# Shifted load buffers, two more of them, an earlier load of the output weights and a shorter split-ahead in a fused transformer kernel

## The chip, the cores and the metric

One core of one Trainium2 chip runs the whole program. The time is device microseconds of one execution. The kernel before was timed three times: 1851.71, 1855.15 and 1855.19 us, median 1855.15 us. One more execution was recorded by the hardware profiler; it took 1854.01 us, and all rows below are from it.

## The reference

Two blocks in a row on 256 tokens of 1024 features, all in fp32:

```python
def first_block(x, c, ada_w, ada_b, ...):
    mod = (silu(c) @ ada_w + ada_b)              # six segments of 1024
    sh1, sc1, g1, sh2, sc2, g2 = split(mod, 6)
    h = rms_norm(x, ln1_g) * (1 + sc1) + sh1
    x = x + g1 * hybrid_mixer(h, w_in, w_out, ...)   # NSA heads and MoBA heads, then @ w_out
    h = rms_norm(x, ln2_g) * (1 + sc2) + sh2
    x = x + g2 * sparse_moe(h, router_w, w1, w2, ...)  # 32 experts, the top 4 of each token
    return x

def sparse_moe(...):    # per expert e and its tokens
    u = hf[toks] @ w1[e] + b1[e]                 # 1024 x 2048
    y = ((lin + 1) * g_ * sigmoid(1.702 * g_)) @ w2[e] + b2[e]   # 1024 x 1024
```

The second block puts 16 learned tokens in front (272 in all) and runs two layers: stick-breaking attention with a squared-ReLU MLP, then a gated linear recurrence with another such MLP, and a last norm.

## The kernel before, in words

Weights are read from HBM once, in one fixed order, by the class `Stream` (from L140). An **item** is one load of 1 MiB into a load buffer of 128 partitions x 2048 fp32; most items are cut into two **units**. `pump` (its DMA is L169, all on SP's queue) issues items in their order. The buffers stand in a ring, and the next item is issued as soon as the ring's first buffer holds only an item that lies before `base`, the first item not yet wholly used. `widen(places, until)` puts more buffers in front of the ring until item number `until`. Dense weights are used as a pair of fp32r tensors: `split_to` writes a unit's high part with a cast on ScalarE (L189) and the rest with a subtraction on VectorE or GpSimd (L191). `get`, called at each use of a unit, first splits up to `ahead` units beyond it, and those two instructions go into the in-order queues of ScalarE and VectorE at that point of the program; where the unit's load has not landed, both queues stand still. `get_raw` hands out an item without a split (modulation and expert weights).

Three stages follow each other:

- **Mixer**, 0 to 251 us (`pre`, `mixer`, `route`). `ada` computes the six segments of the modulation, each from four items (quarters, matmul L436, copy L440); segments 1 and 0 come first, the others are worked off in pieces between other work by `side_to`. `dense_t` and `dense_v` multiply the normed input by the columns of `w_in` (each product three matmuls, L289 to L291 or L488 to L490). The compressed keys and values go through `hid` (matmul L628, copy L632); the norm of a query or key ends with matmul `hb` (L717) and the product `z` (L719). Attention follows, then `w_out`, the router, and the ranks of the tokens within each expert.
- **Experts**, 251 to 1195 us. 17 jobs, 15 of them two experts side by side. A job gathers its tokens (matmul L1407 of a 0/1 matrix `S` with the normed rows, held as `h2h` and `h2l`; scaled and shifted at L1409 into `xs`), multiplies by `w1` (L1442, 8 items for each expert), applies the gate, multiplies by `w2` (L1535, 4 items for each expert) and adds into `h` (L1558 to L1563). There are nine such gathers of eight tiles. 384 items are read. The first 16 are known before the routing; which experts the others hold is read from `ids`.
- **Second block**, 1196 to 1852 us: dense products from split weights. Its first norm (`norm_in`) makes eight `hn_hi` on ScalarE, eight `hn_lo` on VectorE (L1628), eight squares (L1638 on GpSimd, L1640 on ScalarE), and adds them in two chains (L1647, L1650).

The load ring holds four buffers of its own; three arena buffers (r1 to r3) are added until the attention, later the arena tiles that the routing sets free and five split tiles. Scratch tiles of the mixer live in the same arena: `acc` in s4, `alibi` in s6, `z` in r0 and r1, `xn`, `h2h`, `h2l` in s2, s3, s4.

## Time and profile before

| what | value |
|---|---|
| median of three runs | 1855.15 us (1851.71 to 1855.19) |
| profiled execution | 1854.01 us, span 1851.9 us |
| TensorE busy | 1724.2 us, 93% of the span |
| VectorE, ScalarE, GpSimd busy | 718.1, 525.4, 270.6 us |
| bytes moved | 549.63 MB, mean 297 GB/s |

The span runs from the first to the last instruction; the execution's own time is 2.1 us longer. A busy share is an average over the three stages, which have different limits, so the rows below are from short stretches. In a timeline row the first two numbers are the start and the duration in us (of the whole group where xN stands at the end), and a bracket gives the idle time of the engine just before and what ended it. PEclk is the clock granted to TensorE, as a share of its higher level (1.00 is 2.4 GHz, 0.50 is 1.2 GHz).

### The profile page before, as it was taken

The page shows a single profiled execution, that of the slowest core. Times are in us where ns is not written, and L with a number is a line of the kernel's source. Part 1 is how long each engine was busy: PE and PEld are TensorE (multiplying, and loading weights), DVE is VectorE, ACT ScalarE, POOL GpSimd, SP SyncE. Part 2 cuts the span into 40 slices and gives each one's busy share as a digit, 9 for nine tenths or more (in the row PEclk, how much of TensorE's full clock was granted, in tenths as well). Part 3 has the DMA queues.
Part 4 walks back from the last instruction along what each step waited for, and adds up shares of the span by engine and source line. Part 5 has one row for each costly group of instructions (what it writes and reads, how often), then busy time and mean ns, then how long its engine had stood idle before and what let it go on. Part 6 is the DMA issues. An engine that isn't in the chain of part 4 may idle for free. (4 is left out here: it accounts for less than half of the span.)

```text
span 1851.9 us, 25047 instructions
## 1 busy us (share of the span) xinstructions
PE 1724.2 (93%) x9964; PEld 1084.6 (59%) x9964; DVE 718.1 (39%) x1252; ACT 525.4 (28%) x953; POOL 270.6 (15%) x231
## 2 busy tenths in 40 slices
PE   6898989998999999998899989799999999989998
PEld 3776743332334333343443333388889999879986
DVE  3455631322222222221222212355575534876622
ACT  4443320000000000000000000246665544856633
POOL 0000020000000000000000000174433343004442
PEclk7999989999999999999999999999999999999999
DMA  9923889999999999999999999852246555446551
GB/s 344 344 73 114 271 335 398 421 420 422 421 422 421 421 422 420 421 421 421 421 422 420 422 421 421 339 179 81 80 137 180 176 169 173 136 128 182 188 192 72
DMA packets 166952, 549.63 MB, mean 297 GB/s; under 512 B 8656, under 2 KB 101840, under 8 KB 117488
## 3 DMA queue, kind: packets, MB, share of 16 engines
q1 hardware_dynamic: 166208, 546.02, 77.0%
q0 software_dynamic: 432, 1.57, 0.3%
q8 instruction: 80, 1.31, 0.3%
q10 hardware_dynamic: 192, 0.40, 0.1%
q14 instruction: 40, 0.33, 0.0%
HBM read 546.91 MB, written 1.05 MB: 296 GB/s over the span
## 5 line engine op out<-in xcount | busy, mean ns | idle before, releaser
L191 POOL TENSOR_TENSOR wsp<-wraw,wsp 128x1024 fp32r<-128x1024 f32 x91 | 220.0, 2420 | 442.7 <-ACT wsp L189 417.8
L1442 PE MATMUL u<-wraw_s,xs 128*64 128x512 f32 (+1 forms) x848 | 248.6, 600 | 7.3 <-DMA wraw_s<-in_exp_w 7.2
L289 PE MATMUL dps<-hn_hi,wsp 128*128 128x272 f32 (+1 forms) x816 | 239.8, 294 | 7.9 <-DVE gt L2120 3.6
L189 ACT CAST wsp<-wraw 128x1024 fp32r<-128x1024 f32 x210 | 217.1, 1042 | 101.3 <-PE f L2175 46.9
L290 PE MATMUL dps<-hn_lo,wsp 128*128 128x272 f32 (+1 forms) x816 | 235.6, 289 | 4.6 <-DVE hn_lo L1628 4.4
L291 PE MATMUL dps<-hn_hi,wsp 128*128 128x272 f32 (+1 forms) x816 | 235.4, 288 | 0.2 <-DVE wsp L191 0.2
L191 DVE TENSOR_TENSOR wsp<-wraw,wsp 128x1024 fp32r<-128x1024 f32 x119 | 150.9, 1275 | 131.8 <-ACT wsp L189 131.6
L1442 PE MATMUL u<-wraw,xs 128*64 128x512 f32 (+1 forms) x600 | 178.9, 613 | 2.0 <-DMA wraw<-in_exp_w 1.9
L1442 PE MATMUL u<-wraw_r,xs 128*64 128x512 f32 (+1 forms) x600 | 178.5, 602 | 1.4 <-DMA wraw_r<-in_exp_w 1.3
L289 PEld LDWEIGHTS dps<-hn_hi,wsp 128*128 128x128 f32 x816 | 155.9, 191 | 13.3 <-issue 4.9
L290 PEld LDWEIGHTS dps<-hn_lo,wsp 128*128 128x128 f32 x816 | 155.8, 191 | 6.6 <-DVE hn_lo L1628 5.9
L291 PEld LDWEIGHTS dps<-hn_hi,wsp 128*128 128x128 f32 x816 | 155.9, 191 | 0.5 <-DVE wsp L191 0.5
L1442 PEld LDWEIGHTS u<-wraw_s,xs 128*64 128x64 f32 (+1 forms) x848 | 72.1, 140 | 120.7 <-issue 98.6
L1563 DVE SCALAR_TENSOR_TENSOR h<-cb,vec,h 128x256 f32<-128x256 f32 x136 | 59.3, 479 | 178.8 <-PE cb L1559 178.8
L1469 ACT ACTIVATE sg<-gl 128x1024 f32<-128x1024 f32 x17 | 18.0, 1057 | 386.1 <-DVE gl L1468 386.1
L1418 POOL CAST pk<-P 128x128 fp32r<-128x128 f32 x17 | 5.3, 311 | 813.4 <-PE u L1444 810.4
L1535 PE MATMUL y<-wraw,at 128*64 128x512 f32 (+1 forms) x360 | 112.6, 606 | 10.7 <-DMA wraw<-in_exp_w 10.7
L1535 PE MATMUL y<-wraw_s,at 128*64 128x512 f32 (+1 forms) x336 | 108.4, 597 | 11.5 <-DMA wraw_s<-in_exp_w 8.0
L1535 PE MATMUL y<-wraw_r,at 128*64 128x512 f32 x328 | 103.9, 596 | 13.4 <-DMA wraw_r<-in_exp_w 13.4
L1544 DVE SCALAR_TENSOR_TENSOR y<-y,gs 128x1024 fp32r<-128x1024 f32 (+1 forms) x18 | 22.0, 1224 | 215.2 <-ACT y L1543 203.4
L1409 DVE TENSOR_SCALAR xs<-gp,a,vec 128x256 f32<-128x256 f32 (+1 forms) x72 | 37.9, 527 | 164.4 <-PE gp L1407 164.3
L1543 ACT ACTIVATE y<-y,gs 128x1024 fp32r<-128x1024 f32 (+1 forms) x18 | 19.2, 1067 | 245.5 <-PE y L1535 245.5
(499 smaller groups left out, 2903.4 us busy)
## 6 DMA issues: line engine op xcount, KB each, us to landing
wraw_s<-in_exp_w SPq DMA_DIRECT2D x148, 1024.0 KB, 19.8
wraw<-in_exp_w SPq DMA_DIRECT2D x120, 1024.0 KB, 19.8
wraw_r<-in_exp_w SPq DMA_DIRECT2D x116, 1024.0 KB, 19.8
wraw<-in_mlp_w_up SPq DMA_DIRECT2D x32, 1024.0 KB, 5.5
wraw<-in_mlp_w_down SPq DMA_DIRECT2D x32, 1024.0 KB, 4.9
wraw<-in_ada_w SPq DMA_DIRECT2D x14, 1024.0 KB, 5.5
wraw<-in_sb_w_qkv SPq DMA_DIRECT2D x12, 1024.0 KB, 5.5
wraw_r<-in_ada_w SPq DMA_DIRECT2D x10, 1024.0 KB, 11.9
```

The costliest lines, as they stand in the source:

```text
L189: nc.scalar.copy(out=hv, in_=src)
L191: e.tensor_tensor(out=lv, in0=src, in1=lr, op=ALU.subtract)
L289: mm(o, lhsT=wh, rhs=xh, start=first, stop=False)
L290: mm(o, lhsT=wh, rhs=xl, start=False, stop=False)
L291: mm(o, lhsT=wl, rhs=xh, start=False, stop=last)
L1409: nc.vector.tensor_scalar(out=xs[:, k, 0:tot], in0=g, scalar1=self.a2[:, k:k + 1], scalar2=self.mod[:, 24 + k:25 + k], op0=ALU.mult, op1=A ...
L1442: mm(u[n][js], lhsT=xs[:, k, o + j * C:o + j * C + C], rhs=w[:, ns], start=(k == 0), stop=(k == 7))
L1469: nc.scalar.activation(out=sg, in_=g, func=AF.Sigmoid, scale=1.702)
L1535: mm(y[n][js], lhsT=at[:, k, js], rhs=w[:, cs], start=(k == 0), stop=(k == 7))
L1543: nc.scalar.activation(out=yh[:, a], in_=x, func=AF.Copy, scale=gs)
L1544: nc.vector.scalar_tensor_tensor(out=yl[:, a], in0=x, scalar=gs, in1=yh[:, a].bitcast(F32), op0=ALU.mult, op1=ALU.subtract)
L1563: nc.vector.scalar_tensor_tensor(out=h[:, m, META:NT], in0=o, scalar=self.mod[:, 40 + m:41 + m], in1=h[:, m, META:NT], op0=ALU.mult, op1=A ...
```

## The change

- The one-column tile `eps` takes 104 columns. It stands ahead of the load buffers and the arena in each partition, so all of these move from 128 bytes past a multiple of 512 to a multiple of 512.
- The order of the items: modulation segment 0 ahead of the first columns of `w_in` instead of behind; the first two items of `w_out` right behind the last columns of `w_in`, ahead of the four quarters of segment 3; then the other two items of `w_out`, each ahead of two quarters of segment 5.
- One more load buffer, s4, from the start until those last items (`late`); another, s3, from the MoBA projections to the second block. For this `acc` and `alibi` share s6, two small tiles lie in unused columns of `vvt`, and the normed rows are one fp32 tile `h2` in s4 instead of `xn`, `h2h` and `h2l`.
- `ahead` becomes 4 just before the attention rather than in the second product of `w_in`; before it is 2.
- The rows of `h2` are made by two instructions on ScalarE and two on VectorE, instead of six on ScalarE, two on VectorE and two on GpSimd. The gather is two fp32 matmuls a tile instead of four fp32r ones.
- The first norm of the second block: all eight squares on ScalarE, all sums on VectorE.

```diff
         self.h = cp.tile([128, 8, NT], F32, name="h")
         self.tmp = self.pool("tmp", 2)
-        self.eps = cp.tile([128, 1], F32, name="eps")
+        self.eps = cp.tile([128, 104], F32, name="eps")[:, 0:1]
         nc.vector.memset(self.eps, EPS)
         nc.scalar.preload_act_table_set(LNEXP)
...
         w = A["w_in"][0]
-        for q in range(4):
-            add_ada(1, q)
+        for s in (1, 0):
+            for q in range(4):
+                add_ada(s, q)
         add_cols(st, w, 512, 256)
-        for q in range(4):
-            add_ada(0, q)
         cw = A["nsa_cmp_w1"][0]
         for c in range(2):
...
             st.add([(_v("p (k n) -> p k n", k=8), w[:, 2328 + c * 256:2584 + c * 256].rearrange("(k p) n -> p k n", p=128))],
                    [lambda t, m=m: t[:, m * 1024:m * 1024 + 1024] for m in range(2)])
-            more(2)
         wo = A["w_out"][0]
         for c in range(2):
             cs = slice(c * 512, c * 512 + 512)
             st.add([(lambda t, b=b: t.rearrange("p (k n) -> p k n", k=4)[64 * b:64 * b + 64],
                      wo[256 * b:256 * b + 256, cs].rearrange("(k p) n -> p k n", p=64)) for b in range(2)],
                    [lambda t, m=m: t.rearrange("p (k n) -> p k n", k=4)[:, :, m * 256:m * 256 + 256] for m in range(2)])
-            more(2)
+        more(4)
+        self.late = len(st.items)
         for c in range(2):
             add_half(st, wo[:, c * 512:c * 512 + 512], 512, 512)
+            more(2)
         assert not rest
...
             self.queue_moe()
             self.queue_post()
+            self.widen(("s4",), self.late)
             self.widen(("r1", "r2", "r3"), self.early)
...
             for k in range(8):
                 self.square_in(k, h[:, k, X], S)
-            self.acc = self.ar("s4", [128, 2, 256], F32, "acc")
+            both = self.ar("s6", [128, 2048], F32, "both")
+            self.alibi = both[:, 0:1536].bitcast(BF16).rearrange("p (j n) -> p j n", j=8)
+            self.acc = both[:, 1536:2048].rearrange("p (i n) -> p i n", i=2)
             s1, s0 = self.ada(1, pa, "tp"), self.ada(0, self.ps_m, "ot")
             rs = pp.tile([128, 3, S], F32, name="rs1", tag="hr")
...
         kcbd = pp.tile([128, 32], F32, name="kcbd")
-        kr = pp.tile([128, 4, 32], F32, name="kr")
-        hd = pp.tile([128, 4, 32], F32, name="hd")
+        kr, hd = (self.vvt[:, o:o + 128].rearrange("p (j n) -> p j n", j=4) for o in (1024, 640))
         def ckeys():
...
         for i in range(6):
             self.dense_t(0, H, L, S, ev_norm(0, i, 6), 2 * (i // 3))
-            if i == 1:
-                self.st.ahead = 4
         self.fill(len(self.bg))
         heads_rs(0)
...
         self.fill(len(self.bg))
         self.side_to(10)
+        self.st.ahead = 4
         zs.append(self.ar("r1", [128, 8, S], F32, "z"))
         qm, kmo = zs[1][:, 0:4], zs[1][:, 4:8]
...
         for i in range(2):
             self.dense_v(H, L, lambda c, ps, i=i: nc.scalar.copy(out=vm[:, c, i * 256:i * 256 + 256], in_=ps))
+        self.widen(("s3",), self.post_first)
         while state.get("done", -1) < 3:
             self.fill()
...
             self.ms = self.pp.tile([128, 2, 4], F32, name="ms")
-            self.xn = self.ar("s2", [128, 2, 1024], F32, "xn")
+            self.xn = self.h2 = self.ar("s4", [128, 2, 1024], F32, "h2")
             self.lt = self.ps_m.tile([128, 512], F32, name="lt", tag="ss", bufs=1)
             nat = self.pa.tile([128, 2, 512], F32, name="nat", tag="sc")
...
         self.tap("lg", lg)
-        self.h2h = self.ar("s3", [128, 2, 1024], F32R, "h2h")
-        self.h2l = self.ar("s4", [128, 2, 1024], F32R, "h2l")
-        xn = self.xn
-        def rows(q, c, e):
+        def rows(q, c):
             o = slice(q * 512, q * 512 + 512)
-            r, hi, lo, x = rn[:, 0, c:c + 1], self.h2h[:, c, o], self.h2l[:, c, o], self.nat[c][q]
-            if e is nc.scalar:
-                e.activation(out=hi, in_=x, func=AF.Copy, scale=r)
-            elif e is nc.vector:
-                e.scalar_tensor_tensor(out=lo, in0=x, scalar=r, in1=hi.bitcast(F32), op0=ALU.mult, op1=ALU.subtract)
+            r, x = rn[:, 0, c:c + 1], self.nat[c][q]
+            if c:
+                nc.vector.tensor_scalar(out=self.h2[:, c, o], in0=x, scalar1=r, scalar2=None, op0=ALU.mult)
             else:
-                nc.scalar.activation(out=xn[:, c, o], in_=x, func=AF.Copy, scale=r)
-                e.tensor_tensor(out=lo, in0=xn[:, c, o], in1=hi.bitcast(F32), op=ALU.subtract)
-        for q in range(2):
-            for c in range(2):
-                rows(q, c, nc.scalar)
+                nc.scalar.activation(out=self.h2[:, c, o], in_=x, func=AF.Copy, scale=r)
+        rows(0, 0)
+        rows(1, 0)
         mx = pp.tile([128, 2, 8], F32, name="mx")
...
         for c in range(2):
             nc.vector.tensor_scalar(out=sel[:, c], in0=lg[:, c], scalar1=mx[:, c, 3:4], scalar2=None, op0=ALU.is_ge)
-        rows(0, 0, nc.vector)
-        for c in range(2):
-            rows(1, c, nc.gpsimd)
+        rows(0, 1)
         rk = self.ps_m.tile([128, 512], F32, name="rk", tag="ss", bufs=1)
...
         pick, self.early = self.gather(0)
         pick()
-        rows(0, 1, nc.vector)
+        rows(1, 1)
         for _ in range(3):
             self.early.pop(0)()
...
         slots = self.slotp
         if gi:
-            sel = self.ep.tile([128, 2, 256], F32R, name="S", tag="S")
+            sel = self.ep.tile([128, 2, 256], F32, name="S", tag="S")
         else:
-            sel = self.ar("sg", [128, 2, 128], F32R, "S0")
+            sel = self.ar("sg", [128, 2, 128], F32, "S0")
         xs = self.xs[gi] = self.ar(f"s{1 + gi % 2}", [128, 8, 256], F32, "xs")
...
                 g = self.gather_bank()[:, 0:tot]
                 ks = slice(k * 128, k * 128 + 128)
-                for i, x in enumerate((self.h2h, self.h2l)):
-                    for c in range(2):
-                        nc.tensor.matmul(g, lhsT=x[:, c, ks], rhs=sel[:, c, 0:tot], start=(i == c == 0), stop=(i == c == 1))
+                for c in range(2):
+                    nc.tensor.matmul(g, lhsT=self.h2[:, c, ks], rhs=sel[:, c, 0:tot], start=(c == 0), stop=(c == 1))
                 nc.vector.tensor_scalar(out=xs[:, k, 0:tot], in0=g, scalar1=self.a2[:, k:k + 1],
...
             else:
                 sq = self.pc.tile([128, NT], F32, name="sq", tag="nsq", bufs=2)[:, :n]
-            if part == 1 and k % 2 == 0:
-                nc.gpsimd.tensor_tensor(out=sq, in0=src, in1=src, op=ALU.mult)
-            else:
-                nc.scalar.activation(out=sq, in_=src, func=AF.Square)
+            nc.scalar.activation(out=sq, in_=src, func=AF.Square)
             if part == 1:
                 if k < 2:
                     sums.append(sq)
                 else:
-                    e = nc.vector if k % 2 else nc.gpsimd
-                    e.tensor_tensor(out=sums[k % 2], in0=sums[k % 2], in1=sq, op=ALU.add)
+                    nc.vector.tensor_tensor(out=sums[k % 2], in0=sums[k % 2], in1=sq, op=ALU.add)
                 acc = sums[0]
                 if k == 7:
```

On ScalarE, in the first products of `w_in` (`wsp` is a split unit, `wraw` and `wraw_r` load buffers, `sq` and `z` the copies of a product out of PSUM), the order before and then of the change:

```order
L706 ACTIVATE alibi<-once 128x384 x2
L189 CAST wsp<-wraw 128x1024 x2
L189 CAST wsp<-wraw_r_261 128x1024
L697 ACTIVATE sq<-dps 128x256
L698 COPY z<-dps 128x256
```

```order
L709 ACTIVATE both<-once 128x384 x2
L189 CAST wsp<-wraw 128x1024
L700 ACTIVATE sq<-dps 128x256
L701 COPY z<-dps 128x256
L709 ACTIVATE both<-once 128x384
```

Three casts stood in a row ahead of the `sq` and `z` of the product, the third of them of the buffer `wraw_r_261`; now one cast stands there, and the cast of that buffer comes later.

On SP, the loads around the last columns of `w_in` (buffer numbers kept), before and then of the change:

```order
L169 DMA wraw_731<-in_w_in 128x8x256
L169 DMA wraw_886<-in_ada_w 128x2x1024
L169 DMA wraw_954<-in_ada_w 128x2x1024
L169 DMA wraw_1094<-in_w_in 128x8x256
L169 DMA wraw_1258<-in_ada_w 128x2x1024
L169 DMA wraw_1532<-in_ada_w 128x2x1024
L169 DMA wraw_1578<-in_w_out 64x4x512 x2
```

```order
L169 DMA wraw_823<-in_w_in 128x8x256
L169 DMA wraw_s4_895<-in_w_out 64x4x512 x2
L169 DMA wraw_954<-in_w_out 64x4x512 x2
L169 DMA wraw_1095<-in_ada_w 128x2x1024
L169 DMA wraw_1259<-in_ada_w 128x2x1024
L169 DMA wraw_1429<-in_ada_w 128x2x1024
L169 DMA wraw_s4_1541<-in_ada_w 128x2x1024
L169 DMA wraw_1662<-in_w_out 128x4x512
```

The first two loads of `w_out` (each in two halves, x2) now follow the last load of `w_in` directly, where two modulation loads stood ahead of the first of them; the four quarters of segment 3 come behind.

On VectorE, in the routing (`sel` marks the chosen experts, `slot` is a token's rank, `S` the gather's matrix), before and then of the change:

```order
L1080 TENSOR_SCALAR sel<-lg,mx 128x32 x2
L1060 SCALAR_TENSOR_TENSOR h2l<-nat,rn,h2h 128x512
L1094 SCALAR_TENSOR_TENSOR slot<-rk,sel 128x64
L1096 TENSOR_SCALAR slot<-slot 128x64
L1396 TENSOR_TENSOR S_2274<-slot,cst 128x128 x2
L1060 SCALAR_TENSOR_TENSOR h2l<-nat,rn,h2h 128x512
```

```order
L1076 TENSOR_SCALAR sel<-lg,mx 128x32 x2
L1058 TENSOR_SCALAR h_2063<-nat,rn 128x512
L1088 SCALAR_TENSOR_TENSOR slot<-rk,sel 128x64
L1090 TENSOR_SCALAR slot<-slot 128x64
L1389 TENSOR_TENSOR S_2265<-slot,cst 128x128 x2
L1058 TENSOR_SCALAR h_2063<-nat,rn 128x512
```

The instruction ahead of `slot` read `h2h`, which ScalarE makes; the one now there reads only PSUM and the norm's factor.

## Rows read from the trace of the kernel before

**Rows 1.** The page's data rate, in 40 equal slices of 46.3 us, GB/s:

```profile
GB/s 344 344 73 114 271 335 398 421 420 422 421 422 421 421 422 420 421 421 421 421 422 420 422 421 421 339 179 81 80 137 180 176 169 173 136 128 182 188 192 72
```

**Rows 2.** Windows of the whole core; start:end, length, each engine's busy time (instructions), PEclk, DMA share, GB/s:

```profile
62.00:72.00 10.00, 9.79 (x106) 8.00 (x110) 5.20 (x21) 1.76 (x6) 0.78 (x5) 0.81 1.05 391
...
172.00:176.00 4.00, 0.71 (x6) 0.50 (x5) 2.47 (x3) 1.99 (x2) 0.00 (x0) 0.88 0.70 250
176.00:186.00 10.00, 9.67 (x63) 6.89 (x63) 3.36 (x11) 1.84 (x9) 0.00 (x0) 0.71 0.33 106
...
240.00:252.00 12.00, 7.18 (x33) 5.45 (x34) 7.44 (x32) 5.14 (x11) 4.18 (x9) 0.50 1.01 427
...
400.00:575.00 175.00, 158.60 (x683) 56.97 (x679) 36.28 (x61) 8.92 (x11) 1.61 (x6) 0.99 1.01 421
575.00:764.00 189.00, 189.00 (x795) 77.10 (x796) 49.48 (x85) 12.31 (x15) 2.20 (x8) 1.00 1.01 421
764.00:903.00 139.00, 123.84 (x542) 44.65 (x538) 29.88 (x48) 7.74 (x9) 1.07 (x4) 1.00 1.01 421
...
1055.00:1160.00 105.00, 93.61 (x398) 32.40 (x395) 21.20 (x32) 6.68 (x8) 0.83 (x3) 1.00 1.01 421
```

**Rows 3.** Timeline around 60 us: TensorE, ScalarE and VectorE (start, us, what):

```profile
62.21 1.93 PE L628 MATMUL hid<-wraw,once 128*32 128x128 f32 x32 [6.32 <-DVE vvt L632]
...
59.61 1.04 ACT L189 CAST wsp<-wraw_r 128x1024 fp32r<-128x1024 f32 x1 [4.81 <-DMA wraw_r<-in_w_in]
...
60.69 1.22 DVE L191 TENSOR_TENSOR wsp<-wraw_r,wsp 128x1024 fp32r<-128x1024 f32 x1 [4.44 <-ACT wsp L189]
61.83 0.28 DVE L632 COPY vvt<-hid 128x128 f32<-128x128 f32 x1
```

**Rows 4.** Timeline around 174 us: TensorE, ScalarE, VectorE and SP's load issues:

```profile
176.33 1.22 PE L717 MATMUL hb<-hr,spread 128*128 128x256 f32 x2 [3.62 <-DVE z L719]
...
172.45 1.99 ACT L189 CAST wsp<-wraw 128x1024 fp32r<-128x1024 f32 x2 [2.94 <-DMA wraw<-in_w_out]
...
173.53 2.36 DVE L191 TENSOR_TENSOR wsp<-wraw,wsp 128x1024 fp32r<-128x1024 f32 x2 [3.35 <-ACT wsp L189]
...
164.55 2.18 SPq L169 DMA_DIRECT2D wraw<-in_w_out  x2
```

**Rows 5.** Timeline of TensorE at the start, last modulation quarter and first dense product:

```profile
32.40 1.94 PE L436 MATMUL adap<-wraw_r,cond 128*32 128x256 f32 x16 [0.67 <-DMA wraw_r<-in_ada_w]
...
36.75 0.58 PE L289 MATMUL dps<-hh,wsp 128*128 128x256 f32 x1 [0.86 <-ACT hh L565]
```

**Rows 6.** Timeline of VectorE and TensorE in the routing, ahead of the first gather:

```profile
241.66 0.75 DVE L1060 SCALAR_TENSOR_TENSOR h2l<-nat,rn,h2h 128x512 fp32r<-128x512 f32 x1 [0.87 <-ACT h2h L1058]
...
243.25 0.66 PE L1407 MATMUL gp<-S,h2h 128*128 128x128 f32 x2 [1.90 <-ACT xn L1062]
```

**Rows 7.** Timeline of TensorE: an fp32 matmul of 256 columns, and one gather tile:

```profile
171.40 0.59 PE L717 MATMUL hb<-hr,spread 128*128 128x256 f32 x2
...
171.95 0.28 PE L489 MATMUL dps<-wsp,hl 128*128 128x256 f32 x1
...
702.02 0.41 PE L1407 MATMUL gp<-S,h2h 128*128 128x256 f32 x2
702.26 0.41 PE L1407 MATMUL gp<-S,h2l 128*128 128x256 f32 x2
```

**Rows 8.** Windows of the whole core, 4 us each, when the experts begin (columns as before):

```profile
256.00:260.00 4.00, 3.69 (x20) 1.95 (x18) 1.02 (x3) 0.00 (x0) 0.00 (x0) 0.88 0.65 177
...
268.00:272.00 4.00, 4.00 (x15) 1.09 (x13) 0.00 (x0) 0.00 (x0) 0.42 (x2) 1.00 0.55 231
```

**Rows 9.** Timeline at the start of the second block: VectorE and GpSimd:

```profile
1199.37 8.84 DVE L1628 SCALAR_TENSOR_TENSOR hn_lo<-h,vec,hn_hi 128x272 fp32r<-128x272 f32 x8
1208.13 2.09 DVE L1647 TENSOR_TENSOR sq<-sq 128x272 f32<-128x272 f32 x3
...
1202.85 1.63 POOL L1638 TENSOR_TENSOR sq<-h 128x272 f32<-128x272 f32 x2
```

More of the change, by code (lines that the diff above doesn't have):

```diff
@@ L591, in mixer @@
         zs = [self.ar("r0", [128, 8, S], F32, "z")]
-        alibi = self.ar("s6", [128, 8, 384], BF16, "alibi")
+        alibi = self.alibi
         gh = pp.tile([128, 8, 24], F32R, name="gh")
@@ L1157, in gates @@
         nc.vector.tensor_tensor(out=g, in0=self.g4, in1=r.unsqueeze(2).to_broadcast([128, 2, 4]), op=ALU.mult)
-        eg = pool.tile([128, 8, 32], F32, name="geq")
+        eg = pool.tile([128, S], F32, name="gj", tag="gj").rearrange("p (j e) -> p j e", j=8)
         nc.vector.tensor_tensor(out=eg, in0=self.eq, in1=g.rearrange("p c j -> p (c j)").unsqueeze(2).to_broadcast([128, 8, 32]),
@@ L1234, in overflow @@
             h2 = self.ar("s2", [128, 8, S], F32, "h2")
-            xr = self.ar("s1", [128, 2, 1024], F32, "ovr")
-            nc.vector.tensor_tensor(out=xr, in0=self.h2h.bitcast(F32), in1=self.h2l.bitcast(F32), op=ALU.add)
+            xr = self.h2
             for k in range(8):
```

## The prediction

> **What bounds the kernel now.** I read the page's data rate first, because the kernel is three programs in a row with different limits. From slice 8 to slice 25, some 833 us, it stands at 420 to 422 GB/s [rows 1]: the experts are bound by their loads. In the mixer before them it falls to 73 and 114 GB/s, in the second block to 80 to 190: there the transfers are not the limit over long stretches. Then I read windows for the state of TensorE inside those stages [rows 2]. In the experts it is nearly as full as the loads: it has 16.4, 15.2 and 11.4 us without work in 400 to 575, 764 to 903 and 1055 to 1160, 43 us together, and none at all in 575 to 764. So work added to TensorE there is free only up to those 43 us, and faster loads pay only up to them. In the mixer the windows point to two places where TensorE stands still, and the timelines of the engines there say why [rows 3, 4]. Last come the joints between the stages [rows 5, 6, 8, 9].
>
> The profiled execution took 1854.0 us, 1.1 us less than the median of 1855.15. I make the sum against 1854.0. A change under 0.2%, 3.7 us, can't be told from none.
>
> **The start.** The first dense product begins at 36.75, after the last modulation quarter at 32.40, which had itself waited for its load [rows 5]. One 1 MiB load of `w_in` no longer stands ahead of that quarter; at 344 GB/s [rows 1] it is 3.0 us, the most that can be won. Against it, those columns now land last, and need a cast (1.04 us) and a subtraction (1.22 us) [rows 3] before all three matmuls of the first product can run. I take half, -1.5, between -3 and +0.5.
>
> **The shorter split-ahead.** In [rows 3] the reader follows one wait through three in-order queues. ScalarE reaches a cast at 54.8 whose load has not landed and stands for 4.81 us. VectorE has the matching subtraction and stands behind it. Behind that subtraction is a copy of 0.28 us (L632), whose input is ready long before, and TensorE wants that copy: it idles 6.32 us, until 62.21. With two units ahead, the cast of this buffer comes after the next products' copies, so nothing needed early is queued behind it. The whole 6.3 us can go. Afterwards TensorE ran at a mean granted clock of 0.81 over 10 us [rows 2]; between the two levels that is 3.8 us at 1.2 GHz, in which 1.9 us of work at 2.4 GHz was done, so another 1.9 us may return. What is late next are the loads: the DMA share is 1.05 in that window, so the modulation segment that follows at about 66 us can't land sooner, and TensorE would wait for it. I take -5, between 0 and -8.2. Splitting later also holds load buffers longer, by two units, which is one buffer; the added s4 gives just that back, so I cost it at nothing. Without s4 a load would be issued one buffer later.
>
> **The output weights.** [Rows 4] show the same shape at another place. The first load of `w_out` is issued at 164.55 and ScalarE waits for it until 172.45. The subtractions behind run from 173.53 to 175.89, the product `z` (L719) is queued behind them, and TensorE idles 3.62 us until 176.33. Over the next 10 us the granted clock is 0.71 [rows 2], that is 5.8 us at the lower level, costing 2.9. In the new order this load is issued behind the last `w_in` columns, when the transfers run at 73 to 114 GB/s [rows 1] and have room. The price is that segment 3's quarters come behind two items held until the output product is near; the queue may then not pass them, and the last quarters and segment 5 are issued in the last 70 us of the mixer. There the rate is 271 GB/s, under the 421 of the experts [rows 1], so they fit. I take -5.5, between 0 and -6.5.
>
> **The routing.** `h2l` on VectorE starts at 241.66 after a wait on ScalarE's cast, and stands ahead of `slot`; TensorE begins the gather at 243.25 after 1.90 us of idle [rows 6]. The new instruction in that place waits for no cast, and the cast queue of six is two. Its length I take as that of the old one, 0.75. What is won is at most the 1.9, at least nothing; -1.
>
> **The buffer s3.** Once the experts run, loads are issued only as buffers come free, and the channel is not full at first: 177 and 231 GB/s in two windows of 4 us [rows 8], against 421. One more buffer lets the sixteenth known load go out before the ids are there. A load of 1 MiB at 421 GB/s is 2.5 us, the most this can give once; the first of those windows holds 2.3 us of empty channel. -1.5, between 0 and -2.5.
>
> **The gather.** The old tile runs from 702.02 to 702.67, 0.65 us for four matmuls [rows 7]. An fp32 matmul of the same 256 columns (L717, two instructions) starts at 171.40, and the second instruction after it at 171.95; less one short matmul of 0.12 between them (two of the old gather's take 0.24), it holds TensorE for 0.43 us. Two make 0.86, and with the change of operand some 0.9: +0.25 for each of 72 tiles, 18 us. Nearly all of it falls where the loads are the limit and the 43 us of idle time cover it. Not covered are the eight tiles in the first job, when the channel waits for TensorE to free buffers: +2. From both sides: 0 where the loads hide that too, +4 where two gathers show.
>
> **The start of the second block.** Eight `hn_lo` take 8.84 us on VectorE, 1.1 each, while GpSimd runs, and VectorE's sums come at 1208.13 behind them [rows 9]. GpSimd's two first squares are 0.82 each. Four such squares and three sums leave GpSimd and its chain; VectorE gets three more sums at 0.70 [rows 9], 2.1 us. If half of the `hn_lo` run without a neighbour in 0.5 us instead of 1.1, that gives 2.4, and the end of GpSimd's chain no longer counts. -1.5, between -3 and +1.5.
>
> **The 512-byte places.** No row of this trace has a load into a buffer at another place, so the effect is bounded by rates: nothing is lost, and the highest rate that a long window shows is 427 GB/s, with the old places [rows 2], 1.4% over the 421 of the experts. I take nothing, since 427 was reached without the change. Sharing s6 and the columns of `vvt` issues no instruction: nothing, unless a shared tile adds a wait between the copies to `acc` and to `alibi`, which would then show at the place of [rows 3].
>
> The sum is -1.5 - 5 - 5.5 - 1 - 1.5 + 2 - 1.5 = -14.0, so **1840**.
>
> **The rivals.** *Loads into the new places run faster.* If the experts' loads went at 427 GB/s instead of 421, 833 us would become 821, 12 us less, well under the 43 us that TensorE could give up; the time would be 1828. For it: the loads bound 45% of the span. Against: 427 was seen with the old places, in a short stretch, and the steady rate did not move in 18 slices. Chance 0.27. By the Trainium skill ("DMA: Bandwidth & Descriptors", "How a descriptor splits into AXI transactions"), a descriptor that does not start at a multiple of 256 B makes its first transaction start below it and fetch unused bytes; an estimate from that page, 260 beats for 256 in a row of 8 KB, is 1.6%, about 13 us, which gives 1827. That the page's rule holds for the side that is written no run here shows.
>
> *The stalls only move.* The loads around 60 us land no sooner (DMA share 1.05), the split of `w_out` shifts into the attention where it delays another queue, and the routing ends as before; what stays is a third of the gain of 16, less the 2 of the gather: 1850.7. The same would follow if the new `w_out` load found no free buffer before 164. For it: [rows 3] show three waits in a row, and the one in front may only change. Against: both waits are on loads, with an idle queue behind one of them. Chance 0.14.
>
> *The gather becomes the bound (slower).* The rows have no fp32 matmul between the large ones of the experts. If a tile took twice what L717 says, 1.7 us, 72 tiles would add 76 us; the 43 idle us would be eaten and 33 stay. With the other terms, -16, the time would be 1871. It decides from where 72 times the extra exceeds 43 + 16 + 4, that is 0.87 us a tile. Against it stand [rows 7]: the same shape at 0.43. Chance 0.05.
>
> **How the numbers follow.** My forecast as summed, 0.54, with its own range 1834 to 1847; faster loads on top 0.27, around 1828, down to 1816 if the rate gains twice as much, which 43 idle us still allow; stalls moved 0.14, 1846 to 1854; slower 0.05. The range 1824 to 1849 leaves out the lowest part of the second case (0.07), the upper half of the third (0.07) and the fourth (0.05). Faster by over 0.2% means under 1851.4: all of the first two and half of the third, 0.88; the same 0.07; slower 0.05.
>
> **What would show it.** In the new trace: no idle of 6 us ahead of `hid` near 55 us and none of 3.6 us ahead of `hb` near 165; the issue of `w_out` before 130; the experts' stage beginning at about 238 instead of 251; 421 GB/s in the experts (427 would mean the rival); tiles of 0.9 us in the gather, with less idle time of TensorE in the experts' windows and no longer stage; the first dense product of the second block some 1.5 us earlier after the last expert. I am wrong if the experts begin later than 246, if their stage is shorter by over 6 us at the same load count, or if TensorE has no idle time left in them.

## The result and the profile after

| | before | changed |
|---|---|---|
| median of the runs | 1854.38 us (1851.71 to 1855.19) | 1825.28 us (1824.53 to 1830.49) |
| profiled execution, span | 1851.9 us | 1823.3 us |
| mixer, to the first matmul of the experts | 251.3 us | 242.4 us |
| experts, to the end of the last `y` | 943.5 us | 929.8 us |
| second block | 657.1 us | 651.1 us |

The ratio of the times is 0.9852, with an interval of 0.983 to 0.9873: 29 us less where 14 were forecast. The time lies inside the stated range, near its lower end. By stage, the mixer gave 8.9 us, the experts 13.7, the second block 6.0.

The page's data rate of the changed kernel, in 40 slices as in [rows 1]:

```profile
GB/s 354 343 99 143 257 373 395 426 427 427 426 427 427 426 427 426 426 427 426 427 427 427 426 426 427 342 172 82 58 163 183 173 176 172 130 139 179 190 186 69
```

Where the old kernel held 420 to 422 GB/s for 18 slices, this one holds 426 or 427. Windows of the whole core, the columns as in [rows 2]:

```profile
62.00:72.00 10.00, 10.00 (x102) 7.83 (x102) 4.27 (x15) 4.06 (x11) 3.22 (x10) 1.00 1.04 406
97.70:106.00 8.30, 8.27 (x44) 8.30 (x45) 3.73 (x9) 2.04 (x5) 0.00 (x0) 0.59 0.54 123
172.00:176.00 4.00, 4.00 (x32) 2.80 (x32) 1.90 (x5) 0.50 (x3) 0.00 (x0) 1.00 0.54 214
176.00:186.00 10.00, 10.00 (x100) 7.25 (x96) 6.31 (x19) 6.49 (x21) 0.00 (x0) 1.00 0.74 235
...
400.00:575.00 175.00, 168.25 (x723) 65.06 (x723) 43.36 (x75) 11.20 (x14) 1.61 (x6) 1.00 1.01 427
575.00:764.00 189.00, 189.00 (x781) 73.88 (x781) 45.77 (x71) 11.09 (x13) 2.15 (x8) 1.00 1.01 427
764.00:903.00 139.00, 132.47 (x565) 52.69 (x562) 34.05 (x61) 8.97 (x11) 1.61 (x6) 1.00 1.01 426
```

Both stalls of [rows 3, 4] are gone from the stretches where they stood: TensorE is full and at 1.00 in 62 to 72 and in 172 to 186. In the experts TensorE is fuller (6.75 us without work in 400 to 575 against 16.4) at the higher data rate. The second row is new: 8.3 us at a granted clock of 0.59. Timelines of TensorE, and of VectorE, in the changed kernel say what came in the place of the old waits:

```profile
35.54 1.01 PE L449 MATMUL adat<-cst,both 128*128 128x4 f32 x4 [4.83 <-DVE both L441]
...
37.41 0.58 PE L289 MATMUL dps<-hh,wsp 128*128 128x256 f32 x1 [0.86 <-ACT hh L569]
...
57.04 1.08 PE L632 MATMUL hid<-wraw_r,once 128*32 128x128 f32 x32
...
97.73 2.90 PE L776 MATMUL csc<-kcbd,z 128*128 128x32 f32 x16 [2.61 <-DVE ap L692]
...
171.59 0.70 PE L720 MATMUL hb<-hr,spread 128*128 128x256 f32 x2
...
234.27 2.92 PE L1399 MATMUL gp<-S,h 128*128 128x128 f32 x12 [0.96 <-DVE S L1389]
...
699.83 1.13 PE L1399 MATMUL gp<-S,h 128*128 128x256 f32 x4
700.89 3.65 PE L1434 MATMUL u<-wraw,xs 128*64 128x512 f32 x16
```

```profile
32.79 2.36 DVE L191 TENSOR_TENSOR wsp<-wraw_s,wsp 128x1024 fp32r<-128x1024 f32 x2 [11.72 <-ACT wsp L189]
35.07 0.42 DVE L441 COPY both<-adap 128x256 f32<-128x256 f32 x1
...
94.63 1.22 DVE L191 TENSOR_TENSOR wsp<-wraw_s,wsp 128x1024 fp32r<-128x1024 f32 x1
95.77 1.22 DVE L191 TENSOR_TENSOR wsp<-wraw,wsp 128x1024 fp32r<-128x1024 f32 x1
96.90 0.68 DVE L692 TENSOR_TENSOR ap<-vcp,once 128x512 f32<-128x512 f32 x1
...
1176.79 6.28 DVE L1620 SCALAR_TENSOR_TENSOR hn_lo<-h,vec,hn_hi 128x272 fp32r<-128x272 f32 x8
1182.99 2.19 DVE L1635 TENSOR_TENSOR sq<-sq 128x272 f32<-128x272 f32 x6
```

The `hid` that was released at 62.21 starts at 57.04 without a wait, and the `hb` that was released at 176.33 starts at 171.59 without one. But the first dense product starts 0.66 us later than before, not earlier: segment 0's copy (L441) stands on VectorE behind two subtractions whose load now comes last. And at 97.73 TensorE waits for a product of VectorE (L692) that stands behind three subtractions (the last two are shown): with `ahead` raised to 4 at that point, three units are split in one burst.

### The profile page after: what moved, and what is told of

The parts are those of the page before. It is cut to its first block, busy times and chain, and to the rows that moved or that the text cites. A ratio compares the mean times of both kernels' runs of the same rounds, so it can differ in the third digit from the quotient of the medians.

```text
span 1823.3 us, 25032 instructions
## 1 busy us (share of the span) xinstructions
PE 1730.4 (95%) x9964; PEld 1089.8 (60%) x9964; DVE 712.6 (39%) x1255; ACT 524.5 (29%) x953; POOL 263.6 (14%) x222
## 5 line engine op out<-in xcount | busy, mean ns | idle before, releaser
L1434 PE MATMUL u<-wraw_s,xs 128*64 128x512 f32 (+1 forms) x888 | 287.2, 600 | 0.3 <-DMA wraw_s<-in_exp_w 0.3
L1434 PE MATMUL u<-wraw,xs 128*64 128x512 f32 (+1 forms) x600 | 218.4, 606 | 3.6 <-DMA wraw<-in_exp_w 3.5
L191 DVE TENSOR_TENSOR wsp<-wraw,wsp 128x1024 fp32r<-128x1024 f32 x115 | 144.9, 1263 | 125.9 <-ACT wsp L189 125.8
L1434 PEld LDWEIGHTS u<-wraw_s,xs 128*64 128x64 f32 (+1 forms) x888 | 80.4, 140 | 123.5 <-issue 115.5
L1434 PE MATMUL u<-wraw_r,xs 128*64 128x512 f32 (+1 forms) x560 | 151.6, 602 | 1.2 <-DMA wraw_r<-in_exp_w 1.2
L1527 PE MATMUL y<-wraw_s,at 128*64 128x512 f32 (+1 forms) x432 | 135.2, 596 | 6.1 <-PEq L1225 3.2
L1527 PE MATMUL y<-wraw,at 128*64 128x512 f32 (+1 forms) x288 | 98.0, 595 | 6.2 <-DMA wraw<-in_exp_w 6.2
L1434 PEld LDWEIGHTS u<-wraw,xs 128*64 128x64 f32 (+1 forms) x600 | 59.8, 141 | 62.1 <-issue 49.2
L1527 PEld LDWEIGHTS y<-wraw_s,at 128*64 128x64 f32 (+1 forms) x432 | 42.3, 141 | 82.0 <-issue 73.7
## 6 DMA issues: line engine op xcount, KB each, us to landing
wraw_s<-in_exp_w SPq DMA_DIRECT2D x165, 1024.0 KB, 19.1
```

Source lines behind the costliest of these rows:

```text
L191: e.tensor_tensor(out=lv, in0=src, in1=lr, op=ALU.subtract)
L1434: mm(u[n][js], lhsT=xs[:, k, o + j * C:o + j * C + C], rhs=w[:, ns], start=(k == 0), stop=(k == 7))
L1527: mm(y[n][js], lhsT=at[:, k, js], rhs=w[:, cs], start=(k == 0), stop=(k == 7))
```

## The experiments

Each is the changed kernel with one edit, unless it says that it is the kernel before. Times are medians; the kernel before was 1852.8 to 1853.8 us beside them. The changed kernel itself took from 1824.5 to 1830.5 us, so edits worth a few us are read from the stages of the profiled execution. These vary too: runs 2 and 5 have the change's instructions in the mixer, and their experts begin at 239.9 and 241.4 us against its 242.4, so a difference of under 2.5 us in the mixer is not clear. A table of the stages stands in the next section.

**1. The place of the load buffers put back.**

```diff
-        self.eps = cp.tile([128, 104], F32, name="eps")[:, 0:1]
+        self.eps = cp.tile([128, 1], F32, name="eps")
```

> The change with its load buffers back at 128 past a multiple of 512, all else kept. Theory P (the place of the buffers makes the loads faster): steady rate in the experts back to 421 GB/s, their stage about 11 us longer than the 929.8 us of the change, the time about 1836 to 1838. Theory Q (the rate rose for another reason: fewer gather operands, another buffer, less traffic of other engines): 427 GB/s and 1825, no change.

1843.7 us, ratio to before 0.9951 (0.9935 to 0.9967). The windows of this run:

```profile
400.00:575.00 175.00, 165.29 (x702) 60.45 (x699) 39.70 (x68) 10.03 (x12) 1.59 (x6) 0.99 1.01 421
575.00:764.00 189.00, 189.00 (x777) 77.35 (x777) 45.64 (x78) 11.20 (x14) 2.12 (x8) 1.00 1.01 421
```

The rate is 421 GB/s again, with fewer gather operands, the extra buffer and the new order all in. Theory P holds. The place is worth 18 us here by the medians; the profiled executions differ by 19.1: 13.0 in the experts, 5.5 in the mixer, 0.6 in the second block. The part in the mixer was not expected by any theory, and with it the time is 6 us above the expected 1836 to 1838. The loads of the mixer lose more than those of the experts. The windows of its first 60 us, in the change and in this run:

```profile
0.00:60.00 60.00, 40.13 (x364) 30.24 (x364) 20.64 (x46) 27.23 (x56) 1.95 (x11) 0.89 1.05 345
```

```profile
0.00:60.00 60.00, 39.43 (x348) 28.92 (x348) 21.03 (x46) 27.24 (x56) 1.92 (x11) 0.83 1.05 315
```

The DMA records of the traces show a cost for each piece (a run of bytes that one transfer writes). In the experts a piece has 8 KB and takes 309.4 ns in the change and 314.0 here (means). In the first 130 us of the mixer a piece of 1 KB takes 46.2 and 50.5 ns, one of 512 bytes 33.7 and 39.2. So 4 to 6 ns are added to a piece of any of these lengths, and short pieces lose a larger share. In the second block pieces of 1 KB have the same median, 46 ns, at both places; why it costs nothing there, no run shows. In the mixer the later loads end in a wait at the first modulation matmul of segment 2, which has none in the change:

```profile
63.23 1.92 PE L437 MATMUL adap<-wraw_r,cond 128*32 128x256 f32 x16 [3.64 <-DMA wraw_r<-in_ada_w]
```

**2. At 256 past a multiple of 512.**

```diff
-        self.eps = cp.tile([128, 104], F32, name="eps")[:, 0:1]
+        self.eps = cp.tile([128, 40], F32, name="eps")[:, 0:1]
```

> The change with its load buffers at 256 past a multiple of 512. Theory P1 (what counts is a multiple of 256 bytes): 427 GB/s and 1825. Theory P2 (it must be 512): 421 GB/s, about 1837. Theory Q: 427 GB/s, 1825, as in the run with the old place.

1828.0 us (1822.6 to 1830.1), the same as the change. Its first window of the experts:

```profile
400.00:575.00 175.00, 168.28 (x722) 66.38 (x719) 43.90 (x76) 10.81 (x14) 2.12 (x8) 1.00 1.01 427
```

P1 holds: 256 is enough, 512 is not needed.

**3. The kernel before in the new place alone.**

```diff
-        self.eps = cp.tile([128, 1], F32, name="eps")
+        self.eps = cp.tile([128, 104], F32, name="eps")[:, 0:1]
...
-        kr = pp.tile([128, 4, 32], F32, name="kr")
-        hd = pp.tile([128, 4, 32], F32, name="hd")
+        kr, hd = (self.vvt[:, o:o + 128].rearrange("p (j n) -> p j n", j=4) for o in (1024, 640))
...
-        eg = pool.tile([128, 8, 32], F32, name="geq")
+        eg = pool.tile([128, S], F32, name="gj", tag="gj").rearrange("p (j e) -> p j e", j=8)
```

> The kernel before with only the place changed (and, to make the room, the two small tiles in vvt and the shared gj tile). Theory P: 427 GB/s in the experts, their stage about 12 us shorter than 943.5, the mixer's 251.3 and the second block's 657.1 us as before, about 1842. Theory Q: 421 GB/s and 1854.

1836.6 us, ratio 0.9921 (0.9904 to 0.9937).

```profile
400.00:575.00 175.00, 160.03 (x689) 58.49 (x687) 39.15 (x66) 10.29 (x13) 1.59 (x6) 0.99 1.01 427
575.00:764.00 189.00, 189.00 (x805) 75.74 (x805) 49.56 (x80) 11.98 (x15) 2.13 (x8) 1.00 1.01 427
```

One tile made wider (and three small ones moved to make room), and 16 us of the 29 are there, with the order of the work kept. The expected 1842 left out the mixer, 2.8 us shorter, and the second block, 4.4 us shorter with the same instructions (the last section). TensorE is still idle for 15 us in the first window, as before: the loads alone became faster.

**4. The split-ahead raised where it was.**

```diff
             self.dense_t(0, H, L, S, ev_norm(0, i, 6), 2 * (i // 3))
+            if i == 1:
+                self.st.ahead = 4
...
         self.side_to(10)
-        self.st.ahead = 4
```

> The change with the split-ahead set to 4 in the second product of w_in, as before. If the short split-ahead is what removed the 6.3 us of idle ahead of hid: that idle comes back at about 57 us, and the new one of 2.6 us ahead of csc at 98 us goes, since the splits are no longer caught up in one burst there; net +1 to +3 us at the start of the experts, 1826 to 1828. If the idle went for another reason (the extra buffer s4, which lets the load come earlier): none at hid, the start of the experts about 4 us earlier, 1821.

1825.8 us, the experts begin at 244.3. TensorE's timeline:

```profile
61.06 1.93 PE L632 MATMUL hid<-wraw_r,once 128*32 128x128 f32 x32 [4.33 <-issue]
...
101.82 1.94 PE L777 MATMUL csc<-kcbd,z 128*128 128x32 f32 x16 [0.34 <-DVE ap L692]
```

The idle ahead of `hid` is back (the profile names no releaser), and the one ahead of `csc` is gone. So the short split-ahead did remove the first and did make the second; of its gain of some 6 us, 2 are left at the start of the experts, as expected, and the median time does not show them.

**5. The squares of the first norm back on GpSimd.**

```diff
-            nc.scalar.activation(out=sq, in_=src, func=AF.Square)
+            if part == 1 and k % 2 == 0:
+                nc.gpsimd.tensor_tensor(out=sq, in0=src, in1=src, op=ALU.mult)
+            else:
+                nc.scalar.activation(out=sq, in_=src, func=AF.Square)
...
-                    nc.vector.tensor_tensor(out=sums[k % 2], in0=sums[k % 2], in1=sq, op=ALU.add)
+                    e = nc.vector if k % 2 else nc.gpsimd
+                    e.tensor_tensor(out=sums[k % 2], in0=sums[k % 2], in1=sq, op=ALU.add)
```

> The change with the first norm of the second block as before: four squares and three sums on GpSimd. If moving them is what shortened the second block from 657.1 to 651.1 us: 653 to 657 us here, 1827 to 1831 in all. If it did nothing there and the 6 us came from elsewhere (the old-place run of the change had 651.7, the old kernel in the new place 652.7): 651 us and 1825, with hn_lo on VectorE again slow at 1.1 us each.

1827.5 us, the second block 654.6. Its VectorE and its TensorE:

```profile
1175.38 8.83 DVE L1620 SCALAR_TENSOR_TENSOR hn_lo<-h,vec,hn_hi 128x272 fp32r<-128x272 f32 x8
1184.13 2.11 DVE L1639 TENSOR_TENSOR sq<-sq 128x272 f32<-128x272 f32 x3
```

```profile
1187.98 0.39 PE L291 MATMUL dps<-hn_hi,wsp 128*128 128x272 f32 x1 [1.33 <-DVE wsp L191]
```

Eight `hn_lo` take 8.83 us with GpSimd beside them and 6.28 without. At TensorE this is an idle of 1.33 us that the change does not have. The other 2 us of this run's longer second block lie further on, and run 10 shows such a difference without any edit there (the last section).

**6. Without the buffer s3.**

```diff
-        self.widen(("s3",), self.post_first)
```

> The change without the buffer s3: one load buffer fewer in the rest of the mixer and all the experts. If the buffer fills the channel at the start of the experts, as predicted: their stage 1.5 to 2.5 us longer than 929.8, 1827 to 1828. If TensorE's own pace decides there: no difference, 1825.

1827.9 us. From the first `u` to the last job's `y` 914.6 us against 912.2: the buffer is worth 2.4. The change and the seven runs with its code in the experts, this buffer and a fast place (2, 4, 5, 8 to 11) take 911.9 to 913.5, so it is at least 1. The difference does not show at the start of the experts, where TensorE has work enough: the two runs keep step until 430 us, and between 430 and 452 TensorE is without work for 2.9 us here and for 0.8 in the change.

**7. The kernel before with the rows of h2 and the gather in fp32.** The change's hunks on `h2`, its rows, `sel` and the gather, applied to the kernel before:

```diff
-                for i, x in enumerate((self.h2h, self.h2l)):
-                    for c in range(2):
-                        nc.tensor.matmul(g, lhsT=x[:, c, ks], rhs=sel[:, c, 0:tot], start=(i == c == 0), stop=(i == c == 1))
+                for c in range(2):
+                    nc.tensor.matmul(g, lhsT=self.h2[:, c, ks], rhs=sel[:, c, 0:tot], start=(c == 0), stop=(c == 1))
```

> The kernel before with only the rows of h2 in fp32, made by four instructions, and the gather of two fp32 matmuls a tile. Predicted: routing 1 us shorter (first gather at about 242.2 instead of 243.25), tiles of 0.9 us instead of 0.65, idle time of TensorE in the experts down from 47 by about 16 us, and the stage 943.5 us longer by 2: 1855 to 1856. Rival: all tiles hidden, 943.5 and 1853 to 1854. Rival that the gather becomes the bound: over 1860.

1854.2 us, ratio 1.0003 (0.9993 to 1.0012): no difference, so the rival in which all tiles are hidden holds, and not the +2. The mixer is 0.7 us shorter. Windows of this run:

```profile
400.00:575.00 175.00, 162.34 (x695) 59.02 (x693) 38.04 (x63) 8.91 (x11) 1.59 (x6) 0.99 1.01 421
...
764.00:903.00 139.00, 130.35 (x572) 47.76 (x568) 31.05 (x48) 7.74 (x9) 1.06 (x4) 1.00 1.01 421
...
1055.00:1160.00 105.00, 96.50 (x426) 33.80 (x422) 21.20 (x32) 6.68 (x8) 0.82 (x3) 1.00 1.01 421
```

TensorE is without work for 12.7, 8.7 and 8.5 us in these, 30 where it was 43 [rows 2]. First `u` to last job's `y` is 926.5 against 925.9: 0.6 us shows, the loads cover the rest.

**8. The old order of the items.**

```diff
+            more(2)
         wo = A["w_out"][0]
...
-        more(4)
+            more(2)
         self.late = len(st.items)
         for c in range(2):
             add_half(st, wo[:, c * 512:c * 512 + 512], 512, 512)
-            more(2)
```

> The change with the items of w_out and the modulation quarters in the old order. If the early load of w_out is what removed the 3.6 us of idle ahead of hb: it comes back, the experts begin 4 to 6 us later (246 to 248 instead of 242.4), 1829 to 1831. If the extra buffers or the short split-ahead removed it: no idle there, 1825.

1842.4 us, and the experts begin at 256.3, 14 us later, where 4 to 6 were expected. ScalarE and TensorE of this run:

```profile
164.05 1.99 ACT L189 CAST wsp<-wraw 128x1024 fp32r<-128x1024 f32 x2 [5.59 <-DMA wraw<-in_w_out]
...
188.20 1.99 ACT L189 CAST wsp<-wraw 128x1024 fp32r<-128x1024 f32 x2 [6.12 <-DMA wraw<-in_w_out]
```

```profile
167.93 1.22 PE L720 MATMUL hb<-hr,spread 128*128 128x256 f32 x2 [3.85 <-DVE z L722]
...
190.62 1.05 PE L861 MATMUL ot<-ap,vvt 128*64 128x256 f32 x2 [4.05 <-ACT ap L851]
```

Both loads of `w_out` are late here, where before only the first was; why the second is late as well, this run does not show. With the items in the old order the changed kernel's mixer is longer than the old one's 251.3.

**9, 10, 11. Two attempts at a faster version, and both together.** Run 9 issues the first split after segment 0; run 10 raises the split-ahead before the product `vsw`; run 11 does both.

```diff
             self.st.cut = "D"
-            self.st.split_to(2)
             self.st.ahead = 2
             for f in s0:
                 f()
+            self.st.split_to(2)
```

> The change with the first split (units 0 and 1) issued after segment 0 of the modulation instead of ahead of it. In the change the modulation's copy stands behind these two subtractions on VectorE and TensorE idles 4.83 us until 35.54. Theory: the idle goes, the first dense product begins 2 to 3 us before 37.41. If the later part of the mixer follows: experts begin at about 239.5, 1823. If it is bound by loads around 59 us (segment 2): TensorE waits there instead, 242, 1825.

1826.0 us, the experts begin at 243.6. The first dense product starts 3 us earlier, and all of it is lost at segment 2, which waits for its load:

```profile
34.44 0.58 PE L289 MATMUL dps<-hh,wsp 128*128 128x256 f32 x1 [1.51 <-ACT hh L569]
...
59.11 1.94 PE L437 MATMUL adap<-wraw_r,cond 128*32 128x256 f32 x16 [2.06 <-DMA wraw_r<-in_ada_w]
```

```diff
+        self.st.ahead = 4
         self.dense_v(H, L, lambda c, ps: nc.scalar.copy(out=vsw[:, c], in_=ps))
         self.fill(len(self.bg))
         self.side_to(10)
-        self.st.ahead = 4
```

> The change with the split-ahead set to 4 one step earlier, ahead of the product vsw, where ScalarE waits 7.7 us for TensorE. Theory: the three splits that are caught up in one burst ahead of the compressed scores are spread, the idle of 2.61 us ahead of csc and the half clock after it go; experts begin 3 to 4.5 us earlier (238 to 239), 1821 to 1822. Rival: the splits then wait for their load and hold back the copies of vsw; same or later, 1825 or more.

1832.4 us, slower than the change. The rival holds in kind, at `gates` rather than at the copies of `vsw`: ScalarE's cast waits for its load, VectorE's subtraction behind it holds up `gates`, and TensorE stands at `hb`:

```profile
85.10 1.04 ACT L189 CAST wsp<-wraw_s 128x1024 fp32r<-128x1024 f32 x1 [3.22 <-DMA wraw_s<-in_w_in]
```

```profile
87.58 1.22 PE L720 MATMUL hb<-hr,spread 128*128 128x256 f32 x2 [5.06 <-DVE gates L746]
```

The experts begin 2.9 us later. The other 7.8 us of this run's longer span come after that, in stages with the same instructions (the last section).

> Both edits of the last two runs. If they add: first dense product near 35, no idle ahead of csc, experts begin at 236 to 238, 1819 to 1821. If the loads bound the mixer's first 60 us: as the run with the earlier split-ahead alone.

1837.5 us. The edits don't add; segment 2 waits 3.92 us for its load. No version beat the change.

**12. At 224 past a multiple of 512.**

```diff
-        self.eps = cp.tile([128, 104], F32, name="eps")[:, 0:1]
+        self.eps = cp.tile([128, 32], F32, name="eps")[:, 0:1]
```

> The change with its load buffers at 224 past a multiple of 512. If a start off a multiple of 256 costs one more piece for each row, whatever the distance: 421 GB/s as at 128, about 1843. If it costs in proportion to the bytes fetched beside the row: (8416 against 8320 bytes) 416 GB/s, about 1850. If 128 was a special place: 427 GB/s, 1825.

1847.8 us.

```profile
400.00:700.00 300.00, 289.68 (x1191) 114.94 (x1187) 71.29 (x122) 17.87 (x22) 3.19 (x12) 1.00 1.01 420
700.00:1100.00 400.00, 388.69 (x1645) 150.71 (x1645) 96.85 (x155) 24.44 (x29) 3.71 (x14) 1.00 1.01 419
```

Slower than at 128 by a little, 419 to 420 against 421 in the same windows of run 1, and far from 427: between the first two answers, nearer to the first by the rate and to the second by the time (about 1843 and about 1850).

## Why the prediction was right, and where it failed

The table takes the stages apart (us, from the profiled executions; "pace" is from the first `u` to the last job's `y`, which leaves out the experts' end).

| kernel | mixer | experts | their pace | second block |
|---|---|---|---|---|
| before | 251.3 | 943.5 | 925.9 | 657.1 |
| before, new place (3) | 248.5 | 933.3 | 913.3 | 652.7 |
| before, fp32 rows (7) | 250.6 | 945.3 | 926.5 | 655.7 |
| change | 242.4 | 929.8 | 912.2 | 651.1 |
| change, old place (1) | 247.9 | 942.8 | 924.0 | 651.7 |
| change, no s3 (6) | 241.3 | 933.4 | 914.6 | 651.0 |
| change, old order (8) | 256.3 | 929.7 | 912.3 | 651.0 |

*The 512-byte places: the step that failed.* "I take nothing, since 427 was reached without the change" was wrong. The 427 in [rows 2] was a stretch of 12 us; in the experts the new place lifted the steady rate from 421 to 427, and the pace fell by 12.6 us (run 3). That is the first rival as it was sized: 12 us, and 1828 with the rest. It was given 0.27 and is what happened, and the prediction's own sign of being wrong came true: the experts' stage is shorter by 13.7 us, more than the 6 that it allows. The rule of the Trainium skill cited with it ("DMA: Bandwidth & Descriptors", "How a descriptor splits into AXI transactions") names the right boundary, here for the side that is written: 0 and 256 are fast, 128 and 224 slow. Its figure is somewhat high: by an estimate from that page, 260 beats for 256 would be 1.6%, and 421 to 427 is 1.4%; for 224 the same estimate gives 2.7%, and 419 to 420 is 1.7 to 1.9%. I gave the even rate of 18 old slices the weight instead, though all 18 were at the same place and could not speak on it.

A second reading failed with it: that faster loads pay only up to TensorE's idle time. The experts from the first `u` to the last job's `y`, before, in run 3, in run 7 and in the change:

```profile
251.31:1177.21 925.90, 878.71 (x3764) 334.08 (x3764) 218.45 (x363) 58.25 (x71) 10.16 (x35) 1.00 1.01 417
```

```profile
248.53:1161.82 913.29, 872.88 (x3764) 332.08 (x3764) 218.45 (x363) 58.21 (x71) 10.03 (x35) 0.99 1.01 423
```

```profile
250.56:1177.10 926.54, 893.11 (x3764) 343.54 (x3764) 219.41 (x363) 58.17 (x71) 10.08 (x35) 1.00 1.01 417
```

```profile
242.41:1154.58 912.17, 890.06 (x3765) 341.09 (x3764) 219.43 (x363) 58.15 (x71) 10.11 (x35) 1.00 1.01 423
```

In run 3 the same 3764 matmuls need 12.6 us less, and only 6.8 of it is idle time (47.2 to 40.4); the rest was counted as busy by the profile, which models the ends of matmuls. A row that shows TensorE full, as 575 to 764 in [rows 2], does not show that it has no room.

*The mixer.* -13.0 was forecast for its four terms and -8.9 measured. The two terms that failed are the start and what comes behind the shorter split-ahead.

*The start.* -1.5 was forecast, +0.66 measured. The step "those columns now land last" was right and its price too small: the two subtractions stand ahead of the modulation's own copy, 4.83 us of idle. Run 9 shows that mending it gains nothing by itself, since segment 2's load sets the time at 59 us.

*The shorter split-ahead.* From the first dense product to `hid` the change gains 5.8 us (25.46 before, 19.63 now), near the -5. What I did not see is the catching up at `csc`, 2.61 us and then half clock (run 4): from that `hid` to the first `hs` (a sum of squares) of the later products of `w_in` (142.61 before, 140.49 now) 3.0 us are lost again. The stated limit, the loads around 60 us, was real in the old place: there TensorE waits 3.64 us for them, and from `hid` to `csc` run 1 takes 45.8 us against 39.9 before, so that nearly all of the gain is gone. For this term that is the rival in which the stalls only move. In the new place there is no such wait.

*The output weights.* -5.5 was forecast. The wait ahead of `hb` is gone and the clock over 176 to 186 is 1.00. From that first `hs` to the first matmul of the ranks (`rk`, 240.71 before and 232.66 now) 5.9 us are won. Run 8 shows that inside the change the order is worth more, 14 us, since without it the second load of `w_out` is late too.

*The routing.* -1: from `sel` to the gather 1.9 us of idle became 0.96, right.

*The buffer s3.* -1.5 was forecast, 2.4 measured (run 6), at the bound.

*The gather.* From the first matmul of a tile to the next instruction the 72 tiles take 50.7 us in all before and 70.0 in run 7 and in the change: 19 us more, where I had 18. A tile of 256 columns that stands alone is 0.99 us on the mean against 0.69 (from 0.86 to 1.06; the one at 699.83 is among the longest). In run 7 TensorE's idle time took 14 of it (47.2 to 33.4 in the rows above) and 0.6 shows; the rest lies in time counted as busy in both kernels. So the price was right, and the +2 too much. The rival in which the gather becomes the bound needed 0.87 more a tile; it was 0.3.

*The second block.* -1.5 was forecast for the norm; 1.3 of it is seen at TensorE (run 5). The `hn_lo` without a neighbour take 0.79 us each, not 0.5. The profiled pair differs by 6.0. Two pairs with the clock alike put the norm at 1.6 (run 3 against the change) and at 1.2 (before against run 10); the other 4 to 5 us are the clock, and luck (the last section).

So against the forecast's -14, the change without the place gives -9 (run 1), and the place adds 18. By stage run 1 gives -3.4 in the mixer, -0.7 in the experts and -5.4 in the second block, where -13.0, +0.5 and -1.5 were forecast; the last of these is mostly the clock. The range held because the rival was in it, and by 1.3 us at its lower end.

## What to carry to other kernels

Where loads bound a stage, look up the start of the load buffers in a partition early: here a start off a multiple of 256 bytes cost 1.4% of the rate in pieces of 8 KB and 9% of the time of a piece of 1 KB in the mixer, and one wider tile in front gave back more than all the reordering. An even rate over a long time does not show that it is the limit when everything measured shares the same place. In a chain of in-order queues, a cast issued early for a load that has not landed delays whatever stands behind it (6.3 us at `hid`, 3.6 at `hb` in the kernel before). Moving it gains only if the next load in the chain is already there, and only if the splits put off do not come in one burst ahead of something that is wanted (2.61 us at `csc`).

## What the runs showed of the hardware

*The granted clock after a short idle.* Ahead of the last job's `y` TensorE stands for 3.1 to 3.5 us in every run, with the same instructions behind. TensorE's timeline in the change and in run 10:

```profile
1154.58 1.94 PE L1527 MATMUL y<-wraw_s,at 128*64 128x512 f32 x8 [3.18 <-PEq L1225]
```

```profile
1158.00 3.68 PE L1527 MATMUL y<-wraw_s,at 128*64 128x512 f32 x8 [3.10 <-PEq L1225]
```

The same eight matmuls take 1.94 us and 3.68. In runs 1, 6 and 7 the clock over the next 5 us was 0.66 to 0.68, in runs 3, 10 and 11 it was 0.50, in the others 0.73 to 1.00; to the end of the last `y` it is 17.2 to 20.0 us. The same happens in the second block. Windows of 20 us that begin some 30 us after the last `y`, over the same products, before, in run 3, in the change and in run 10:

```profile
1225.00:1245.00 20.00, 16.16 (x109) 14.76 (x108) 10.85 (x15) 9.80 (x20) 15.72 (x18) 0.91 0.49 158
```

```profile
1212.00:1232.00 20.00, 17.20 (x128) 15.48 (x127) 6.86 (x15) 11.36 (x22) 16.94 (x19) 1.00 0.48 158
```

```profile
1202.00:1222.00 20.00, 17.16 (x126) 15.30 (x125) 6.86 (x15) 11.38 (x24) 16.89 (x18) 1.00 0.49 158
```

```profile
1208.00:1228.00 20.00, 16.16 (x108) 14.68 (x107) 10.70 (x14) 10.15 (x21) 14.88 (x17) 0.91 0.49 158
```

The kernel before and run 10 get through fewer matmuls at a clock of 0.91, run 3 and the change through more at 1.00; 170 us after the last `y` the clocks of these four are 0.91, 1.00, 1.00 and 0.91 again. It does not go by the code: run 3 has the instructions of the kernel before in this block, and run 10 those of the change. The block took 657.1 and 655.9 us at the lower clock, 652.7 and 651.1 at the higher. So 4 to 5 us of a difference between two executions of this kernel can be the clock after idle places, with no edit near them, and so much of the second block's 6.0 is not the change's. What decides whether the clock falls after such a wait, no run shows.
